# Layer 1 of a two-layer encoder: query rows in natural order, the dilation-16 weights transposed by VectorE in 32x32 blocks, V loaded by class, a new rank table

## The chip, the cores and the metric

The kernel runs on one core of a Trainium2 chip. The metric is device time in microseconds (us) of one launch; the reshaping of inputs and outputs by the host isn't in it. The engines have short names: PE is TensorE's matmul, PEld its weight load, DVE VectorE, ACT ScalarE, POOL GpSimd, SP the queue that issues most DMA transfers. SBUF is the working memory of 128 partitions, PSUM the memory that matmuls write, in banks of 512 float32 a partition.

## What is computed

A sequence of 512 tokens of width 1024, float32, goes through two layers. Each layer adds a normed token mixer and a normed SwiGLU to `x`. Layer 0 mixes by neighbourhood attention on an 8 x 64 grid; layer 1, which the change edits, by dilated attention:

```python
DIL_GROUPS = ((128, 1), (512, 4), (2048, 16))        # window, dilation; 16 heads of 64
for g, (window, dil) in enumerate(DIL_GROUPS):
    radius = window // (2 * dil)                       # 64 in each group
    # queries and keys of one residue mod dil form a sub-sequence of length s // dil
    o, lse = banded_attention(q * HEAD_DIM ** -0.5, k, v, radius, slopes * dil)
alpha = softmax(stack(lses), axis=0)                   # merge the three groups by their denominators
o = einsum('gbsh,gbshd->bshd', alpha, stack(outs))
return o @ w_o
```

With 512 tokens, dilation 4 has four classes (residues) of 128 tokens, and dilation 16 has sixteen of 32 tokens. A dilation-16 class lies within one dilation-4 class. Scores outside the window or of another class get -1e30 and so weight 0.

## The kernel before

**Products.** Every large product is a Winograd scheme with seven products in place of eight (class `Seven`, line 527 on). An operand is split into a high and a low fp32r part (`split`, lines 484 and 485: ACT copies, DVE subtracts), and three matmuls (`mm3`, lines 499 to 501) make one. A unit of layer 1 (`qk_unit`, line 799) makes the queries and keys of one pair of heads `j` (8 pairs) in one group `g` (0, 1, 2 for dilations 1, 4, 16): 24 units. Its weights `r_d` are loaded by the SP queue, their sums are formed by POOL (lines 567 to 573), and its results leave PSUM through `sink` (line 809): step 0 is the first half of the queries (ACT line 812, DVE line 813), step 1 and 2 are the keys (lines 818, 820, 823), step 3 the second half of the queries (ACT line 825). `pieces` says where each part goes: a list of pairs of a destination and a view of the source.

**Row order.** In group 0 the queries are stored in four blocks of 128 tokens, rolled by 64 tokens, and in each block by residue: 32 rows of residue 0 mod 4, 32 of residue 1, and so on (`q4`, line 1324). Hence the source is read with a stride of four, in three pieces per half. In groups 1 and 2 queries and keys are stored by residue mod 4 and in a class by position (`by_token`, line 1310). The rows of attention output and of the final result have the order of group 0, and the host undoes it.

**Attention of layer 1.** For a pair `j` the scores come in chunks. `scores_a` serves dilation 1, `scores_b` (line 1408) both dilated groups: for each class `c` one 128x128 product for dilation 4 and one for dilation 16, side by side. `softmax_pair` adds the bias (custom DVE operation, line 1381) and takes the exponential (ACT, line 1382). The row statistics of the two halves lie in different row orders, so `send` and `swapped` (lines 1340 to 1355) pass them through a small DRAM tile `sw`: one transfer there, four back. `weights` makes the merge factors (lines 1364 to 1372). `weighed` (line 1464) scales the weights by them (ACT, line 1469), transposes eight 128x128 blocks per head and half on PE (line 1479, against `ident`) into two PSUM banks, and copies one bank to SBUF by ACT, one by DVE (line 1480). `values` (line 1482) multiplies V: line 1488 for dilation 1, line 1494 for the dilated groups, which add to the same PSUM bank `o`, 64 partitions per head. `keep` splits and stores the result (lines 1169 to 1172). V itself is made before, stored to DRAM as `vd` and loaded by quarters of four heads (`v_load`, line 1453, transfer in line 1457). After the last pair the output product `yo` follows, and `load_block` (line 1565) loads the residual rows in the order of group 0.

**Order of the work.** The program is written unit after unit (`run`, `between`, `done`): chunks of scores and of `weighed` and `values` of earlier pairs are put between the products of the current unit. The order on each engine isn't the written one. `Order.pin` (line 370) plans it: it schedules the instructions by rank with a table of costs, forward and backward, twenty times, takes the ranks of turn `FIRST`, and then changes ranks by `TABLE`. An entry `(what, engine, lo, hi, turn, by)` names instructions by planned start time or by index, and shifts their ranks. The resulting order is pinned for every engine and for all of the program, so one table ranks layer 0, both feed-forward parts and layer 1. Engines and DMA queues work strictly in this order.

## Time and profile before

| | |
|---|---|
| runs | 1437.45, 1436.01, 1437.60 us; median 1437.45 |
| profiled execution, own time | 1437.08 us |
| its span, first to last instruction | 1435.3 us |
| PE, DVE, ACT, POOL busy | 1393.2, 1190.4, 913.8, 532.0 us |
| TensorE clock granted, mean | 0.994 |
| layer 1's units and attention | about 700 to 1045 us of the span |

Busy is the time in which an engine worked on at least one instruction. A matmul's duration in a group of instructions includes its passage through the array, during which the next ones run; what a run of them costs is read from the distance of their starts or from the chain. The chain that ended last is followed back from the last instruction, at each step to what released it.

### The profile page before, as it was taken

What the parts mean: (1) busy time and instruction counts of PE and PEld (TensorE: products, weight loads), DVE (VectorE), ACT (ScalarE), POOL (GpSimd) and SP (SyncE); (2) the same over time, 40 slices, a digit from 0 to 9 for tenths busy, and PEclk for the clock granted to TensorE, in tenths of its full rate; (3) what the DMA queues carried; (4) which work ended last, traced back from release to release, by engine and by line L of the source; (5) the groups of instructions that cost most, each with busy time, mean ns of one, the idle gap of its engine ahead of it and who ended that gap; (6) DMA issues with size and microseconds to landing.
All of it is one profiled execution on the core that took longest, in us unless ns stands there. A gap on an engine that the chain in (4) does not pass through costs nothing.

```text
span 1435.3 us, 27816 instructions
## 1 busy us (share of the span) xinstructions
PE 1393.2 (97%) x10714; PEld 1301.9 (91%) x10714; DVE 1190.4 (83%) x1891; ACT 913.8 (64%) x1853; POOL 532.0 (37%) x394
## 2 busy tenths in 40 slices
PE   8999999999999999999999999999999999999997
PEld 7989978999999888999999999989988999999886
DVE  7789968899998888998688777777759888898986
ACT  6489965555555667745567787788775645455664
POOL 3745526454330001676453334343216443440001
PEclk9999999999999999999999999999999999999999
DMA  7257588778324674455333353433766897845662
GB/s 248 95 200 185 175 294 224 233 227 219 118 91 141 211 234 169 157 170 187 120 103 91 112 171 97 142 96 91 251 200 240 243 250 221 247 127 169 198 213 96
DMA packets 86646, 253.21 MB, mean 176 GB/s; under 512 B 19313, under 2 KB 31601, under 8 KB 84465
## 3 DMA queue, kind: packets, MB, share of 16 engines
q1 hardware_dynamic: 77696, 197.69, 41.5%
q0 software_dynamic: 8672, 53.48, 14.8%
q8 instruction: 84, 1.38, 0.4%
q14 instruction: 50, 0.40, 0.1%
q10 hardware_dynamic: 144, 0.26, 0.0%
HBM read 229.24 MB, written 68.29 MB: 207 GB/s over the span
## 4 chain that ended last, share of the span: by engine, by line
PE 77%; DVE 12%; ACT 4%; issue 3%; DMA 2%; POOL 1%; POOLq 0%; DVEq 0%; SPq 0%; ACTq 0%
PE gu L499 8%; PE gu L501 8%; PE gu L500 8%; PE pp_d L499 5%; DVE wring L485 4%; PE pp_d L501 4%; PE pp_d L500 4%; PE yd_s L499 3%; PE yd_s L500 3%; PE yd_s L501 3%; PE yd_pp L500 2%; PE yd_pp L499 2%; PE yd_pp L501 2%; PE yo L501 2%; PE yo L499 2%
## 5 line engine op out<-in xcount | busy, mean ns | idle before, releaser
L499 PE MATMUL gu<-rxa,wring 128*128 128x256 f32 x704 | 193.6, 281 | 1.5 <-DVE mem L978 1.3
L501 PE MATMUL gu<-rxa,wring 128*128 128x256 f32 x704 | 190.4, 278 | 2.2 <-DVE wring L485 2.2
L500 PE MATMUL gu<-rxa,wring 128*128 128x256 f32 x704 | 192.3, 277 | 0.0
L485 DVE TENSOR_TENSOR wring<-r_d,wring 128x1024 fp32r<-128x1024 f32 x112 | 142.9, 1283 | 39.9 <-ACT wring L484 39.2
L485 DVE TENSOR_TENSOR wring<-raw,wring 128x1024 fp32r<-128x1024 f32 (+1 forms) x120 | 156.0, 1302 | 16.8 <-ACT wring L484 16.2
L484 ACT ACTIVATE wring<-raw 128x1024 fp32r<-128x1024 f32 x120 | 122.4, 1020 | 61.2 <-PE gu L500 31.2
L484 ACT ACTIVATE wring<-r_d 128x1024 fp32r<-128x1024 f32 x112 | 115.8, 1040 | 33.2 <-PE gu L500 9.5
L499 PEld LDWEIGHTS gu<-rxa,wring 128*128 128x128 f32 x704 | 131.3, 188 | 4.5 <-DVE mem L978 2.3
L501 PEld LDWEIGHTS gu<-rxa,wring 128*128 128x128 f32 x704 | 130.3, 188 | 3.3 <-DVE wring L485 3.2
L500 PEld LDWEIGHTS gu<-rxa,wring 128*128 128x128 f32 x704 | 131.9, 188 | 0.2
L499 PE MATMUL pp_d<-rxa,wring 128*128 128x256 f32 x384 | 108.2, 284 | 2.4 <-ACT wring L484 0.9
L500 PE MATMUL pp_d<-rxa,wring 128*128 128x256 f32 x384 | 106.6, 280 | 0.0
L501 PE MATMUL pp_d<-rxa,wring 128*128 128x256 f32 x384 | 105.5, 280 | 0.0
L707 POOL TENSOR_TENSOR rs_yd<-v_yd,consts 128x1 f32<-128x1 f32 x8 | 8.9, 1115 | 259.2 <-DVE v_yd L705 259.2
L499 PE MATMUL gu<-rxc,wring 128*128 128x256 f32 x352 | 98.5, 282 | 5.2 <-ACT wring L484 3.3
L500 PE MATMUL gu<-rxc,wring 128*128 128x256 f32 x352 | 99.0, 282 | 1.4 <-DVE rxc L724 1.4
L501 PE MATMUL gu<-rxc,wring 128*128 128x256 f32 x352 | 98.7, 282 | 0.4 <-DVE wring L485 0.3
L484 ACT ACTIVATE wring<-r_gu 128x1024 fp32r<-128x1024 f32 x60 | 63.5, 1058 | 50.6 <-PE gu L500 23.5
L484 ACT ACTIVATE rxc<-mem 128x512 fp32r<-128x512 f32 (+2 forms) x95 | 60.6, 645 | 52.2 <-PE yd_pp L500 21.1
L485 DVE TENSOR_TENSOR wring<-r_gu,wring 128x1024 fp32r<-128x1024 f32 x60 | 76.9, 1284 | 13.2 <-ACT wring L484 12.9
L567 POOL TENSOR_TENSOR r_d<-r_d 128x512 f32<-128x512 f32 x24 | 34.0, 1415 | 132.2 <-DVE wring L485 97.2
L567 POOL TENSOR_TENSOR r_gu<-r_gu 128x512 f32<-128x512 f32 x20 | 33.8, 1692 | 127.7 <-DVE wring L485 92.8
(477 smaller groups left out, 5240.7 us busy)
## 6 DMA issues: line engine op xcount, KB each, us to landing
wsum<-wd POOLq DMA_DIRECT2D x24, 1408.0 KB, 10.8
r_d<-dil_qk SPq DMA_DIRECT2D x48, 512.0 KB, 4.0
raw<-wg SPq DMA_DIRECT2D x24, 512.0 KB, 6.0
raw<-wu SPq DMA_DIRECT2D x24, 512.0 KB, 8.3
wsum<-wsum POOLq DMA_DIRECT2D x8, 1408.0 KB, 7.9
raw<-wsum SPq DMA_DIRECT2D x22, 512.0 KB, 4.3
r_gu<-wg SPq DMA_DIRECT2D x20, 512.0 KB, 5.9
r_gu<-wu SPq DMA_DIRECT2D x20, 512.0 KB, 8.4
```

Of the source, the lines that this page charges most:

```text
L484: act.activation(h, src, AF.Copy)
L485: dve.tensor_sub(l, src, h.bitcast(F32))
L499: i = pe.matmul(o, s[0], m[0], start=start, stop=False, skip_group_check=True)
L500: pe.matmul(o, s[0], m[1], start=False, stop=False, skip_group_check=True)
L501: pe.matmul(o, s[1], m[0], start=False, stop=stop, skip_group_check=True)
L567: self.added = e[0].tensor_add(q[0], q[0], q[2])
L707: pool.tensor_tensor(r, v, mhalf, op=ALU.pow)
```

## The change

It does six things, all but the last in layer 1.

1. Group 0 stores its queries in natural order: one piece in the first half, two in the second. Groups 1 and 2 store a dilation-4 class of 128 rows as four runs of 32, one for each residue of the position mod 4 (`p r s a`: class, run, place). Their queries' sum in step 0 is made in four DVE instructions in place of one (`pairs`).
2. With that order each dilation-16 class is a run of 32 rows and of 32 columns, so the 128x128 block of weights is zero off its four 32x32 diagonal blocks. Its transpose is the transpose of each 32x32 block in its own place, for which `dve.transpose` is called, SBUF to SBUF: four of them per head in place of four PE transposes, one PSUM bank and one DVE copy. Dilation 4 and dilation 1 stay on PE.
3. The dilated value products write the bank `o` in natural token order: for a class, columns with a stride of 16 in place of runs of 32.
4. `v_load` loads V of the two dilated groups in four transfers of 32 partitions each, one for each run.
5. `swapped` passes the statistics through a tile of 512 rows of four values: one transfer of small pieces and four by run, in the one direction or the other. `load_block` loads two pieces of 64 rows in place of four or eight pieces. The bias arrays have other contents and the same shape; the host's reordering of the output goes.
6. `FIRST` and `TABLE` are replaced whole.

```diff
-FIRST, TABLE = 2, (
-    (0, 5, 957181, 993986, 6, 279), (0, 5, 741028, 748810, 14, 3080), (2, 0, 10189, 10217, 0, -1138),
...
+FIRST, TABLE = 11, (
+    (0, 5, 49788, 92169, 1, -42768), (2, 5, 5932, 6125, 0, -961), (2, 5, 7102, 7152, 0, -1660),
...
+        def pairs(o, v):
+            return [(o, v)] if len(o.shape) < 4 else [(o[:, :, n], v[:, :, n]) for n in range(o.shape[2])]
+
...
-                sums = in_turn([dve.scalar_tensor_tensor(o, view(left), 0.125, o, op0=ALU.mult, op1=ALU.add)
-                                for o, view in qd[0]])
+                sums = in_turn([dve.scalar_tensor_tensor(o, v, 0.125, o, op0=ALU.mult, op1=ALU.add)
+                                for o, view in qd[0] for o, v in pairs(o, view(left))])
...
-        return v.rearrange("p (m r) -> p r m", r=4)
+        return v.rearrange("p (a s r) -> p r s a", s=4, r=4)
...
-            q4 = qs.rearrange("p (b r n) -> p b r n", b=4, r=4)
-            qd = [[(q4[:, 0, :, 16:], places(0, 16)), (q4[:, 1], places(16, 32)), (q4[:, 2, :, :16], places(48, 16))],
-                  [(q4[:, 2, :, 16:], places(0, 16)), (q4[:, 3], places(16, 32)), (q4[:, 0, :, :16], places(48, 16))]]
+            qd = [[(qs[:, 64:320], whole)], [(qs[:, 320:], some(whole, 0, 192)), (qs[:, :64], some(whole, 192, 64))]]
...
-            q3, k3 = (v.rearrange("p (r n) -> p r n", r=4) for v in qk[i])
-            qd = [[(q3[:, :, 16:80], by_token)], [(q3[:, :, 80:], places(0, 48)), (q3[:, :, :16], places(48, 16))]]
-            kd = [[(k3[:, :, 64 * n:64 * n + 64], by_token)] for n in range(2)]
+            q3, k3 = (v.rearrange("p (r s a) -> p r s a", s=4, r=4) for v in qk[i])
+            qd = [[(q3[..., 4:20], by_token)], [(q3[..., 20:], some(by_token, 0, 12)), (q3[..., :4], some(by_token, 12, 4))]]
+            kd = [[(k3[..., 16 * n:16 * n + 16], by_token)] for n in range(2)]
...
+    sw = [dpool.tile([SEQ, 4], F32, name=f"sw{i}") for i in range(4)]
+    def swapped(out_, in_, d, back):
+        rows = d.rearrange("(b p) k -> p b k", b=4)
+        by_class = d.rearrange("(a s r) k -> s a (r k)", s=4, r=4)
+        if not back:
+            nc.sync.dma_start(rows, in_.rearrange("p (b k) -> p b k", b=4))
+        for n in range(4):
+            v = slice(32 * n, 32 * n + 32)
+            nc.sync.dma_start(*((by_class[n], in_[v]) if back else (out_[v], by_class[n])))
+        if back:
+            nc.sync.dma_start(out_.rearrange("p (b k) -> p b k", b=4), rows)
...
-            nc.sync.dma_start(v, src.rearrange("(t p) c -> p t c" if g == 0 else "(p t) c -> p t c", t=NT))
+            if g == 0:
+                nc.sync.dma_start(v, src.rearrange("(t p) c -> p t c", t=NT))
+            else:
+                for n in range(4):
+                    nc.sync.dma_start(v[32 * n:32 * n + 32], src.rearrange("(a s r) c -> s a r c", s=4, r=4)[n])
...
-        for n in range(2):
+        for i in range(4) if a_b else ():
+            dve.transpose(pt[:, 512 + i * P:512 + i * P + P], part(*b8[4 + i]))
+        for n in range(2 - a_b):
             t = bank("t", f"t1_{j}")
...
-                    pe.matmul(o[64 * hd:64 * hd + 64].rearrange("p (b r n) -> p b r n", b=4, r=4)[:, :, c],
+                    pe.matmul(o[64 * hd:64 * hd + 64].rearrange("p (a s r) -> p r s a", s=4, r=4)[:, c],
...
     def load_block(xt, b):
...
+        nc.sync.dma_start(xt[:64], spill[1][(b + 3) % 4, 64:])
+        nc.sync.dma_start(xt[64:], spill[1][b, :64])
```

More of the change, by code (lines that the diff above doesn't have):

```diff
@@ L1310, in by_token, with some @@
     def by_token(v):
-        return v.rearrange("p (m r) -> p r m", r=4)
-    def places(i, n):
-        return lambda v: by_token(v)[:, :, i:i + n]
+        return v.rearrange("p (a s r) -> p r s a", s=4, r=4)
+    def some(view, i, n):
+        return lambda v: view(v)[..., i:i + n]
     xm, qk, us = mixer_operands(rxb), {}, {}
@@ L1330, in unit_of @@
             qk[i] = next(f_), next(f_)
-            q3, k3 = (v.rearrange("p (r n) -> p r n", r=4) for v in qk[i])
-            qd = [[(q3[:, :, 16:80], by_token)], [(q3[:, :, 80:], places(0, 48)), (q3[:, :, :16], places(48, 16))]]
-            kd = [[(k3[:, :, 64 * n:64 * n + 64], by_token)] for n in range(2)]
+            q3, k3 = (v.rearrange("p (r s a) -> p r s a", s=4, r=4) for v in qk[i])
+            qd = [[(q3[..., 4:20], by_token)], [(q3[..., 20:], some(by_token, 0, 12)), (q3[..., :4], some(by_token, 12, 4))]]
+            kd = [[(k3[..., 16 * n:16 * n + 16], by_token)] for n in range(2)]
         us[i] = qk_unit((a["dil_qk"][g, 0, j], a["dil_qk"][g, 1, j]), xm, next(p5_), next(w22_), f"d{i}", (qd, kd))
         return us[i]
-    sw = [dpool.tile([P, 16], F32, name=f"sw{i}") for i in range(4)]
-    def swapped(out_, in_, d, n):
-        nc.sync.dma_start(d[:, :4 * n], in_)
-        for k in range(4):
-            nc.sync.dma_start(out_[32 * k:32 * k + 32].rearrange("p (i s) -> p i s", s=n),
-                              d[:, n * k:n * k + n].rearrange("(i p) s -> p i s", i=4))
+    sw = [dpool.tile([SEQ, 4], F32, name=f"sw{i}") for i in range(4)]
[9 more added lines that the diff above has]
+            nc.sync.dma_start(out_.rearrange("p (b k) -> p b k", b=4), rows)
     def by_kind(v):
@@ L1354, in send @@
         few = stats[j][2]
-        swapped(few[:, 48 - 16 * t:64 - 16 * t], stats[j][t], sw[2 * t + j % 2], 4)
+        swapped(few[:, 48 - 16 * t:64 - 16 * t], stats[j][t], sw[2 * t + j % 2], t)
     def weights(j):
@@ L1565, in load_block @@
     def load_block(xt, b):
-        rows = spill[1].rearrange("t (m r) d -> r (t m) d", r=4)
-        for r in range(4):
-            if b:
-                nc.sync.dma_start(xt[32 * r:32 * r + 32], rows[r, 32 * b - 16:32 * b + 16])
-            else:
-                nc.sync.dma_start(xt[32 * r:32 * r + 16], rows[r, 112:128])
-                nc.sync.dma_start(xt[32 * r + 16:32 * r + 32], rows[r, 0:16])
+        nc.sync.dma_start(xt[:64], spill[1][(b + 3) % 4, 64:])
+        nc.sync.dma_start(xt[64:], spill[1][b, :64])
     then(exp, AF.Exp)
@@ L1617, in _dist @@
 def _dist():
-    r, n = np.divmod(np.arange(P), 32)
-    q = (4 * n + r)[:, None]
     k = np.arange(P)
+    q = k[:, None]
     dp, dn = np.abs(q + 64 - k), np.abs(q - 64 - k)
     prev, next_ = np.where(dp <= 64, -dp, NEG), np.where(dn <= 64, -dn, NEG)
-    d = 4 * np.abs(k[:, None] - (k + 16) % P)
+    n, a = np.divmod(k, 32)
+    m = 4 * a + n
+    d = 4 * np.abs(m[:, None] - (m + 16) % P)
     return np.concatenate([prev, next_, np.where(k < 64, NEG, prev), np.where(k < 64, next_, NEG),
@@ L1668 @@
     y = r.results[0]["out"]
-    return np.ascontiguousarray(y.reshape(4, 4, 32, D).transpose(0, 2, 1, 3).reshape(1, SEQ, D))
+    return np.ascontiguousarray(y.reshape(1, SEQ, D))
```

121 rows, old and new, of the table c are left out of this document.

## The prediction, made before the changed kernel was run

> **What bounds the kernel now.** I read the first part of the profile page first, then busy time by stage, because the change touches only layer 1's mixer and an average over the span says little of it.
>
> ```profile
> PE 1393.2 (97%) x10714; PEld 1301.9 (91%) x10714; DVE 1190.4 (83%) x1891; ACT 913.8 (64%) x1853; POOL 532.0 (37%) x394
> PE 77%; DVE 12%; ACT 4%; issue 3%; DMA 2%; POOL 1%; POOLq 0%; DVEq 0%; SPq 0%; ACTq 0%
> ```
> ```profile
> core 0: us, PE busy (x) PEld busy (x) DVE busy (x) ACT busy (x) POOL busy (x), PEclk, DMA share, GB/s
> 245.00:560.00 315.00, 310.77 (x2266) 292.39 (x2265) 280.73 (x361) 182.44 (x303) 87.20 (x56) 0.99 0.59 185
> 700.00:765.00 65.00, 62.42 (x528) 60.44 (x527) 52.61 (x89) 40.76 (x94) 33.78 (x24) 1.00 0.38 112
> 765.00:1045.00 280.00, 274.11 (x2474) 258.03 (x2474) 214.11 (x510) 222.48 (x586) 101.31 (x75) 1.00 0.43 135
> 1045.00:1075.00 30.00, 30.00 (x180) 24.32 (x179) 14.13 (x22) 19.99 (x38) 3.06 (x3) 1.00 0.64 186
> ```
>
> The first line of the page is busy time by engine, the second the chain that ended last by engine. TensorE (PE) is busy 97% of the span and carries 77% of the chain. In the stages that the change touches, 700 to 1075 us, it is busy 62.42 + 274.11 + 30.00 = 366.5 of 375 us: 8.5 us idle. VectorE (DVE) is busy 214 of 280 us in the main stage, so 66 us are open there; ScalarE has 57. The row 245 to 560 shows a stage in which DVE is busy 280.73 of 315 us (89%) and PE still 98.7%. So in this kernel a microsecond taken from PE inside 765 to 1045 comes off the end, and work given to DVE is paid only where it delays PE.
>
> **The transposes that leave TensorE.** Per head and weight half the kernel transposes eight 128x128 blocks on PE and copies two banks out, one by ScalarE (ACT), one by DVE. In the dilated half the second bank (dilation 16) goes to DVE altogether: 16 heads x 4 = 64 transposes leave PE, 16 DVE copies go, 64 DVE transposes come.
>
> ```profile
> L1479 PE MATMUL t<-ident,mem 128*128 128x128 f32 x256 | 38.0, 274 | 1.2 <-ACT mem L1469 1.2
> L1480 DVE COPY mem<-t 128x512 f32<-128x512 f32 x32 | 22.0, 689 | 20.1 <-PE t L1479 19.9
> L1494 PE MATMUL o<-mem 128*64 128x128 f32 x256 | 17.2, 274 | 0.0
> ```
> ```profile
> 823.14 0.87 PE t L1479 x8
> 829.36 1.75 PE o L1494 x32
> 921.95 6.46 DMA r_d<-dil_qk
> 1204.99 9.02 DMA raw<-wg
> ```
> ```profile
> 822.75 0.28 PE L500 MATMUL pp_d<-rxa,wring 128*128 128x256 f32 x1
> 822.87 0.28 PE L501 MATMUL pp_d<-rxa,wring 128*128 128x256 f32 x1
> 822.98 1.04 PE L1479 MATMUL t<-ident,mem 128*128 128x128 f32 x8
> 823.82 0.39 PE L499 MATMUL pp_d<-rxb,rxc 128*128 128x256 f32 x1
> 824.05 0.28 PE L500 MATMUL pp_d<-rxb,rxc 128*128 128x256 f32 x1
> ```
>
> The group's mean of 274 ns is a latency; matmuls are pipelined. What a transpose costs PE is read from the chain (second fence): eight take 0.87 us, 109 ns each. Hence 64 x 0.109 = **-7.0 us**. The timeline in the third fence gives the change between kinds of matmul: from 822.87 to 824.05 are 1.18 us, which hold two ordinary steps of 0.12 us (822.75 to 822.87 is one) and the eight transposes, so 1.18 - 0.24 - 0.87 = 0.07 us for going in and out. Where the second bank was a visit of its own that goes too: 16 x 0.07 = 1.1 us at most, nothing at least; I take half, **-0.6 us**.
>
> On DVE 16 x 0.689 = 11.0 us leave. No DVE transpose stands in the trace. The nearest rows are operations of 64, 128 and 256 elements a partition:
>
> ```profile
> L813 DVE SCALAR_TENSOR_TENSOR memc<-pp_d,memc x24: 207/214/281, 694.0 to 1019.8; 128x64 f32<-128x64 f32 x16, 128x128 f32<-128x128 f32 x8
> L813 DVE SCALAR_TENSOR_TENSOR mem<-pp_d,mem x16: 407/418/445, 707.9 to 1005.3; 128x256 f32<-128x256 f32 x16
> L820 DVE TENSOR_TENSOR mem<-mem,pp_d x16: 405/418/422, 721.1 to 1013.3; 128x256 f32<-128x256 f32 x16
> L823 DVE TENSOR_TENSOR mem<-memc,pp_d x16: 496/609/702, 725.5 to 1015.5; 128x256 f32<-128x256 f32 x16
> L823 DVE TENSOR_TENSOR memc<-memc,pp_d x8: 406/415/421, 708.9 to 1032.3; 128x256 f32<-128x256 f32 x8
> L818 ACT ACTIVATE mem<-pp_d x16: 364/384/387, 720.2 to 1012.9; 128x256 f32<-128x256 f32 x16
> L818 ACT ACTIVATE memc<-pp_d x8: 366/383/385, 705.0 to 1029.3; 128x256 f32<-128x256 f32 x8
> ```
>
> The slowest of the first row, 281 ns, is its 128-element form. Bounds for a transpose: 214 ns (the 64-element form) and 689 ns (the 512-element copy). I take 281, the row of the same size: 64 x 0.281 = 18.0 us, at the ends 13.7 and 44.1. So DVE gains 7.0 us, at worst 33. The Trainium skill, "VectorE: DVE Perf Modes", section "The three transpose paths", gives 311 ns for a 128x128 bf16 block on VectorE, whose blocks of 32x32 are transposed each in its place; by it DVE would gain 8.9 us in place of 7.0, and no run here shows it. The new DVE transposes wait for ACT's scaling of the weights; behind them on DVE stand the weight splits of L485, which PE's products need. Before, a copy stood there that waited for the same scaling and then for PE (19.9 us in all for both halves), so no wait is added and about half of one goes; its gain on PE is counted at nothing, since the stage's PE has little idle time to give.
>
> **Query sinks.** For dilation 1 three pieces become one in the first half and two in the second: per head pair DVE goes from 214 + 281 + 214 to one operation of 418 ns, -0.29 us; ACT loses three instructions. For the two dilated groups the DVE sum is cut in four because of its four-dimensional pattern: 4 x 214 in place of 418 ns, +0.44 us, 16 times. Together 16 x 0.44 - 8 x 0.29 = +4.7 us of DVE. With the transposes that is +11.7 us: 226 of 280 us, still under the 89% of the stage shown above. Strides grow from 4 to 16 elements in the dilated reads. In the rows of L818 and L820 against the contiguous L823 `memc` row, reading PSUM with the stride of 4 costs nothing (384 against 383, 418 against 415 ns); a strided SBUF operand costs (609 against 415), and is strided already. I take 0. The sum is also 0.44 us later for whoever needs the `left` bank: if every one of 16 were exposed, +7.0 us; none, 0.
>
> ```profile
> PEld pp_d L499 <- DVE mem L813: 0.2, 1, 0.2
> POOL r_d L567 <- DMA r_d<-dil_qk: 22.2, 4, 10.5
> ```
>
> In the list of waits PE's weight loads waited once for this line, 0.2 us. Cover is there (scores and values stand between), so I take two exposures: **+0.8 us**.
>
> **The value products** write the same columns to PSUM with a stride of 16 elements in place of runs of 32. No matmul of the trace writes so. L1494 takes 1.75 us per head pair (32 records, two column halves side by side): 16 records in line, 109 ns each for 128 columns, 0.85 ns a column. The bounds are 0 (the same columns through the same array, nothing makes them shorter) and a doubling, 8 x 1.75 = +14.0 us, more than the factor 1.47 that a strided SBUF operand costs DVE. ACT reads strided PSUM without loss at (384 - 226)/192 = 0.82 ns an element (226 is the 64-element row of L812 below), a new line of PSUM each time; that is as fast as these matmuls write. I take 0. The Trainium skill says the contrary, "Advanced Engine Details and Errata", section "PSUM Cachelines": a pattern that isn't contiguous slows matmuls significantly. By it the sum would lose the most of what it gains; it is the first rival below.
>
> **DMA.** Each quarter of V loads two dilated groups in four transfers each in place of one: +24, six of these loads inside 700 to 1075. The swap of statistics keeps five transfers and as many packets (512 of 16 bytes, 128 of 64), only the direction of the small ones differs. The residual rows lose 12.
>
> ```profile
> L1457 SPq DMA_DIRECT2D mem<-vd x9: 337/383/958, 829.6 to 1019.6; - x9
> mem<-spill SPq DMA_DIRECT2D x12, 128.0 KB, 2.9
> mem<-vd SPq DMA_DIRECT2D x9, 512.0 KB, 4.7
> mem<-sw SPq DMA_DIRECT2D x64, 2.0 KB, 3.0
> L812 ACT ACTIVATE memc<-pp_d x24: 201/226/277, 693.0 to 1018.7; 128x64 f32<-128x64 f32 x16, 128x128 f32<-128x128 f32 x8
> ```
>
> An issue costs the SP queue 0.383 us. A quarter's load puts 6 more ahead of whatever follows, 2.3 us; three quarters come in the stage, 6.9 us if PE stood for all. Queued behind are the weight loads `r_d`, and POOL already waited 22.2 us for them; the chain has one such load on it (921.95, 6.46 us, just behind a V load). Transfers of 128 KB on 32 partitions land in 2.9 us (the residual rows), four against one of 4.7 us. I take **+0.5 us**. For the swap I take 0: the trip is about 2.9 + 3.0 us and a unit of products (84 matmuls of 0.12 us) covers 10; a doubled landing would still be hidden in the middle pairs and exposed only for the last, where PE has the output product. The 12 issues saved lie under a PE that is busy 30.00 of 30 us: 0.
>
> **The order.** The new table re-ranks the whole program, layer 0 and both feed-forward parts too. PE idles 1435.3 - 1393.2 = 42 us; a new order can win or lose some of it. I take 0, with 4 us to either side: the loads that stand on the chain cost it 6 to 9 us each, and most of their time PE has other work.
>
> **Sum:** -7.0 - 0.6 + 0.8 + 0.5 = -6.3 us. The profiled execution took 1437.08 us (span 1435.3), 0.4 below the median of 1437.45: **1430.8 us**, or 0.44% less. Its own range: 1424.5 (both banks' switching, -8.1, half of the stage's 8.5 us idle closed) to 1434.5 (half of the late sinks exposed, +2.7, and 1 us more of issues).
>
> **Rivals.**
> 1. *Strided PSUM writes slow the value products; slower.* One mechanism, at L1494: with a factor f on its 14.0 us the total is 1430.8 + 14.0 (f - 1). The gain is gone from f = 1.45; at the doubling, 1444.8. For it: no row shows a strided matmul write, and adding to PSUM reads and writes. Against: the strided reads of L818 above. 15%, of which 4 with an f too small to cost the whole gain.
> 2. *No gain, the stage is held elsewhere.* Weight splits on ACT and DVE and the loads of `r_d` set the pace; the holes in PE grow by what it was given: about 1437, with the order's 4 us from 1435 to 1441. For it: 12% of the chain is DVE. Against: 8.5 us of idle PE in 375. 12%.
> 3. *DVE becomes the bound:* transposes at 689 ns, DVE at 214 + 33 + 5 = 252 of 280 us (90%), like the stage shown at 89% where PE still keeps 98.7%. PE would lose 1 to 2% more of 280 us: 1434 to 1437. 5%.
> 4. *A load comes late in the new order:* the six added issues stand before `r_d`, or the table places a weight load late; one more hole of 6.5 to 9 us as at 921.95 and 1204.99: 1437 to 1440; two of them, 1444 to 1449. 4% each.
>
> Forecast: 60%. About 0.2%, 2.9 us, is what a measurement of this kernel tells from no change. Faster: 57 of the 60, 4 of rival 1, 3 of rival 3: 64%. Within: 3 + 3 of rival 1 + 8 of rival 2 + 2 of 3 + 4 of 4 = 20%. Slower: 8 + 4 + 4 = 16%. The range that leaves 2 in 10 out reaches to 1422 below (the forecast's lower end with an order that wins 2.5) and 1442 above (rival 1 to f = 1.8, rivals 2 and 3 whole, rival 4 with one hole).
>
> **What will show it.** L1479 with 192 records in place of 256; 64 DVE transposes near 281 ns; PE busy some 7 us less over the span and the mixer's stage shorter by that. Wrong if the 32 records of L1494 take clearly more than 1.75 us (rival 1), if PE's idle time between 700 and 1075 grows by 5 us or more (rivals 2 and 3), if a wait of PE for L813 or of POOL and ACT for `r_d` grows by microseconds (late sinks, rival 4), or if a stage that was not edited moves by more than 4 us.

## The result: 1.65% slower

The changed kernel took 1460.95 us (median; 1458.22 to 1464.29), the kernel before 1437.53 us on the same chip: 1.0165 times, 95% interval 1.0141 to 1.0188, 23.4 us more. The forecast was 1430.8 us, its range ended at 1442. The profiled execution has a span of 1459.8 us, against 1435.3.

The first part of the page of the changed kernel, busy time by engine, and its chain:

```profile
PE 1401.4 (96%) x10650; PEld 1304.1 (89%) x10650; DVE 1200.5 (82%) x1971; ACT 911.0 (62%) x1829; POOL 548.9 (38%) x394
PE 17%; DVE 4%; DMA 2%; issue 1%; ACT 1%; POOL 1%; POOLq 0%; DVEq 0%; SPq 0%; ACTq 0%
```

What matters is PE: 64 matmuls fewer than before (10650 against 10714), and 8.2 us *more* busy time (1393.2 before). More work can't be the reason; a slower clock can be a part of it, which the last section takes up. The shares of this page's chain add up to 26%, those of the kernel before to 99%: here the page follows the chain over a part of the span only, so I read it by windows, below.

What was edited behaves as foreseen. The groups of the four edited operations, with count, busy us and mean ns:

```profile
L1490 DVE STREAM_TRANSPOSE mem<-mem 128x128 f32<-128x128 f32 x64 | 15.9, 288 | 2.5 <-ACT mem L1482 2.1
L1494 PE MATMUL t<-ident,mem 128*128 128x128 f32 x192 | 36.2, 283 | 2.1 <-ACT mem L1482 2.0
L1495 DVE COPY mem<-t 128x512 f32<-128x512 f32 x16 | 11.0, 689 | 10.0 <-PE t L1494 10.0
L1509 PE MATMUL o<-mem 128*64 128x128 f32 x256 | 18.5, 275 | 0.0
```

192 transposes are left on PE, DVE has 64 at 288 ns (281 was assumed), 16 copies are gone, and the value products with the strided PSUM write keep their 275 ns. The edited mixer's stage, in the stretches that the prediction used:

```profile
700.00:765.00 65.00, 64.11 (x548) 62.28 (x547) 47.51 (x98) 40.44 (x88) 34.42 (x23) 1.00 0.35 107
765.00:1045.00 280.00, 270.99 (x2378) 253.52 (x2377) 223.66 (x561) 215.94 (x550) 111.58 (x78) 0.99 0.47 129
1045.00:1075.00 30.00, 30.00 (x184) 24.81 (x183) 17.77 (x44) 22.40 (x50) 0.66 (x2) 1.00 0.74 210
```

PE idles 9.9 us of these 375, after 8.5 before. The stretches are fixed in time and the changed kernel reaches its work later, so they show how busy the stage is and not how long it takes. Nothing here is 23 us. So I looked where each stage begins and ends, by the first and last matmul of its PSUM tile. Here the gate and up products `gu` of both layers, before and after: shortest, median and longest in ns, then the start of the first and of the last. Layer 0's first is in the row of `rxc`, layer 1's last in the row of `rxa,wring`.

```profile
L501 PE MATMUL gu<-rxa,wring x704: 276/276/388, 257.6 to 1327.1; 128*128 128x256 f32 x176
L499 PE MATMUL gu<-rxc,wring x352: 276/276/420, 240.7 to 1299.4; 128*128 128x256 f32 x176
```
```profile
L504 PE MATMUL gu<-rxa,wring x704: 276/276/417, 265.2 to 1351.9; 128*128 128x256 f32 x176
L502 PE MATMUL gu<-rxc,wring x352: 276/276/581, 249.0 to 1322.3; 128*128 128x256 f32 x176
```

Layer 0's mixer, of which no line was edited, hands over at 249.0 in place of 240.7. The same reading of the other tiles gives the lengths of the stages:

| stage, us | before | after | difference |
|---|---|---|---|
| start to first `gu` (layer 0's mixer, not edited) | 240.7 | 249.0 | +8.3 |
| to the first product of the dilated V, `vp_d` (layer 0's feed-forward part, not edited) | 333.1 | 329.5 | -3.6 |
| to the last transpose `t` (layer 1's mixer, edited) | 492.6 | 498.9 | +6.3 |
| to the last `gu` (second gate and up, not edited) | 260.7 | 274.5 | +13.8 |
| to the last product `yd_s` of the second down stage (not edited) | 99.6 | 99.6 | 0 |

18.5 of 24.8 us arose where only the rank table acts. Two places make most of them. By windows (columns: PE, PEld, DVE, ACT and POOL busy, then PE's granted clock, the transfer engines' share, GB/s), before and then after:

```profile
130.00:160.00 30.00, 29.76 (x249) 27.58 (x250) 27.32 (x75) 28.06 (x74) 13.93 (x18) 1.00 0.66 180
1110.00:1150.00 40.00, 39.90 (x343) 39.25 (x342) 36.07 (x50) 24.01 (x42) 19.60 (x13) 1.00 0.78 226
1150.00:1200.00 50.00, 49.69 (x432) 49.31 (x431) 44.61 (x55) 24.55 (x43) 21.89 (x17) 1.00 0.79 222
```
```profile
130.00:160.00 30.00, 26.50 (x197) 23.72 (x195) 23.04 (x67) 20.55 (x57) 13.51 (x14) 0.94 0.58 158
1110.00:1150.00 40.00, 36.73 (x311) 35.71 (x309) 33.15 (x46) 22.69 (x40) 25.51 (x17) 1.00 0.69 202
1150.00:1200.00 50.00, 42.44 (x347) 41.58 (x348) 33.87 (x43) 23.07 (x40) 14.95 (x12) 0.93 0.80 216
```

In 1150 to 1200 the changed kernel issued 347 matmuls where the one before issued 432, and the clock was 0.93. In the first place 249 - 197 = 52 matmuls are missing, in the second (both rows) 775 - 658 = 117. At 0.12 us each, the usual distance of two, that is an estimated 6 and 14 us. The chain of waits of the changed kernel through that place, and PE's timeline across the hole (start, duration, engine, line, operation, and in brackets what it waited for):

```profile
1138.20 15.62 DMA r_gu<-wg
1153.91 1.06 ACT wring L487
...
1156.03 0.21 PE gu L502
...
1158.29 0.12 PE gu L503
...
1173.63 9.30 DMA raw<-wg
```
```profile
1148.33 0.28 PE L503 MATMUL gu<-rxa,wring 128*128 128x256 f32 x1
1155.02 0.58 PE L502 MATMUL gu<-rxc,wring 128*128 128x256 f32 x1 [6.40 <-ACT wring L487]
```

A weight load of 512 KB took 15.62 us to land; PE stood still for 6.4 us; and when it resumed, a matmul came every 0.21 us in place of 0.12 until 1158. The loss is the hole and then the slow restart.

Around both places POOL issues transfers that were not described so far. The down stage needs sums of its weight quarters, and the transfers form them themselves: 32 of them, of 1.4 MB each (16 per layer, `wsum`, in `wd_sums`, line 1010 of the kernel before), half of which add to what is in memory. They run long ahead of the down stage, next to the weight loads of everything else. The transfers issued at 129 to 143 us, before and after (KB each, median us to landing):

```profile
wsum<-wd POOLq DMA_DIRECT2D x1, 1408.0 KB, 13.7
r_n<-na_qk SPq DMA_DIRECT2D x2, 512.0 KB, 8.3
```
```profile
wsum<-wd POOLq DMA_DIRECT2D x1, 1408.0 KB, 13.4
r_n<-na_qk SPq DMA_DIRECT2D x2, 512.0 KB, 11.4
```

In the kernel before SP issues one weight load of `r_n` at 129.13, ahead of the sum at 130.19, and one behind it, at 131.18; in the changed order both go out at 130.78, behind the sum of 129.61. The same view of the second place, 1130 to 1156 us, before and after:

```profile
wsum<-wd POOLq DMA_DIRECT2D x3, 1408.0 KB, 11.8
raw<-wg SPq DMA_DIRECT2D x3, 512.0 KB, 8.7
```
```profile
wsum<-wd POOLq DMA_DIRECT2D x4, 1408.0 KB, 13.7
r_gu<-wg SPq DMA_DIRECT2D x1, 512.0 KB, 15.6
```

There the changed order issues four weight loads within 2.2 us (1137.83 to 1140.01), between three sums of 1129.5 to 1133 and a fourth at 1142.26; they land after 11.3 to 20.6 us. The kernel before spreads six loads over 1133.6 to 1155, between sums of 1117 to 1121 and others from 1145 on; they land after 7.2 to 10.4 us in the median of each kind.

### The profile page after: what moved, and what is told of

Read it like the earlier page. It is cut to its first block, busy times and chain, and to the rows that moved or that the text cites. A ratio compares the mean times of both kernels' runs of the same rounds, so it can differ in the third digit from the quotient of the medians.

```text
span 1459.8 us, 27793 instructions
## 1 busy us (share of the span) xinstructions
PE 1401.4 (96%) x10650; PEld 1304.1 (89%) x10650; DVE 1200.5 (82%) x1971; ACT 911.0 (62%) x1829; POOL 548.9 (38%) x394
## 5 line engine op out<-in xcount | busy, mean ns | idle before, releaser
L488 DVE TENSOR_TENSOR wring<-raw,wring 128x1024 fp32r<-128x1024 f32 x120 | 156.3, 1308 | 19.5 <-ACT wring L487 18.3
L502 PEld LDWEIGHTS gu<-rxa,wring 128*128 128x128 f32 x704 | 132.8, 190 | 8.5 <-DVE mem L982 3.5
L504 PEld LDWEIGHTS gu<-rxa,wring 128*128 128x128 f32 x704 | 131.8, 190 | 4.4 <-DVE wring L488 4.4
L503 PEld LDWEIGHTS gu<-rxa,wring 128*128 128x128 f32 x704 | 133.1, 190 | 0.1
L502 PE MATMUL gu<-rxc,wring 128*128 128x256 f32 x352 | 97.8, 280 | 8.9 <-ACT wring L487 8.4
L503 PE MATMUL gu<-rxc,wring 128*128 128x256 f32 x352 | 97.7, 280 | 0.2 <-DVE rxc L727 0.2
L504 PE MATMUL gu<-rxc,wring 128*128 128x256 f32 x352 | 97.7, 279 | 0.0
L570 POOL TENSOR_TENSOR raw<-raw 128x512 f32<-128x512 f32 x24 | 41.2, 1718 | 126.6 <-DVE wring L488 111.9
```

Of the source, the lines that this page charges most:

```text
L488: dve.tensor_sub(l, src, h.bitcast(F32))
L502: i = pe.matmul(o, s[0], m[0], start=start, stop=False, skip_group_check=True)
L503: pe.matmul(o, s[0], m[1], start=False, stop=False, skip_group_check=True)
L504: pe.matmul(o, s[1], m[0], start=False, stop=stop, skip_group_check=True)
L570: self.added = e[0].tensor_add(q[0], q[0], q[2])
```

## Experiments

Theory after this reading, A: the edit is worth about what was forecast, and the new rank table loses 20 us and more, because it issues weight loads where they share the transfer engines with the sums. Rival B: the edited code itself loses time (its strided writes, its extra transfers), and the stages around it only show the consequences. Rival C: the table loses time on the compute engines, and the loads aren't the cause.

To part code from order, every kernel below has the rank of each instruction written into it, so that the order on each engine can be chosen freely:

```diff
-        for _ in range(times):
-            starts, _, end = self.run(rank, False)
...
-        order = self.run(rank, False)[1]
+        rank = given_ranks(len(self.all))
+        order = [sorted((k for k in range(len(self.all)) if self.engine[k] == e), key=lambda k: (rank[k], k))
+                 for e in range(len(ENGINES))]
```

"Old order" means that all instructions which both kernels have stand on each engine in the order of the kernel before, and the new ones where those stood that they replace. All runs, each against the kernel before on the same chip:

| run | code, order | us | ratio to before [95%] |
|---|---|---|---|
| changed kernel | new, new | 1460.95 | 1.0165 [1.0141, 1.0188] |
| e1 | new, old (writes of the swap spread) | 1446.69 | 1.0049 [1.0030, 1.0068] |
| e2 | old, new | 1474.57 | 1.0241 [1.0221, 1.0261] |
| e3 | new, old (writes of the swap together) | 1440.26 | 1.0022 [1.0009, 1.0036] |
| e4 | as e3, V loads, swap and query sums as few as before | 1434.61 | 0.9973 [0.9962, 0.9985] |
| e5 | as e3, all transposes on PE | 1443.44 | 1.0037 [1.0023, 1.0051] |
| e6 | as e3, query sums in one | 1438.48 | 1.0000 [0.9980, 1.0020] |
| e7 | new, new, no sums of down weights | 1438.72 | 0.9991 [0.9977, 1.0005] |
| e8 | new, old, no sums of down weights | 1436.68 | 0.9973 [0.9958, 0.9989] |
| e9 | new; new order in layer 0 only | 1443.88 | 1.0031 [1.0019, 1.0043] |
| e10 | new; new order up to the second gate and up | 1454.34 | 1.0107 [1.0076, 1.0139] |
| e11 | as e3, V in one transfer | 1460.05 | 1.0138 [1.0121, 1.0156] |
| e12 | as e11, swap in one transfer a side | 1455.12 | 1.0110 [1.0091, 1.0129] |
| e13 | new, new, sums with an eighth of the bytes | 1439.75 | 1.0001 [0.9987, 1.0016] |
| e14 | as e3, V in one transfer from plain rows | 1438.20 | 0.9989 [0.9975, 1.0004] |
| e15 | as e3, swap in one transfer a side | 1438.20 | 0.9987 [0.9972, 1.0002] |

### Code or order: e1 and e2

The edit is the ranks alone: the changed code with the old order, and the code before with the new order.

> The changed code, every instruction that it shares with the kernel before put in exactly the order of the kernel before on each of the five queues; the new instructions stand in the places of those that they replace (a DVE transpose where the PE transpose of the same block stood). Theory A (the loss is the new rank table: stages whose code is the same carry 18 of the 24.5 us, and the edit itself still saves PE work): the layer-0 mixer is back at 241 us, the second gate and up stage at 235 us, and the whole lies at 1427 to 1436 us. Theory B (the edit costs, by strided PSUM writes, smaller transfers or later DVE work, and holds the later stages up too): 1450 to 1461 us, with the second gate and up stage still near 249 us.

> The code before, in the order of the changed kernel (163 of 10250 shared PE instructions are displaced, by 28 places at most, where the removed transposes come back). Theory A: slower than the kernel before by 18 to 31 us, 1455 to 1468, with the same holes as the changed kernel in the layer-0 mixer (first gate and up product near 249 us) and in the second gate and up stage (about 249 us). Theory B: 1434 to 1442 us.

Measured: 1446.69 and 1474.57 us (before: 1439.17). The new order costs the old code 35.4 us. With it, layer 0 hands over at 248.8 us and the second gate and up stage ends at 1365.8: the holes belong to the order, not to the edited lines. In the old order the changed code hands over at 240.9, as before. So most of the loss is the table's; B is left with at most 7.5 us. Neither run lies in a range that was expected: e1 is 11 us over A's and under B's, e2 is 7 us over A's. (The expectations count the second gate and up stage from its own first product: by that count it takes 232.7 us before, 247.0 after, 233.3 in e1 and 248.5 in e2.) The 12 us between +35.4 and +23.4 arise in layer 1's mixer: from the first `vp_d` to the last `t` it takes 511.3 us in e2 and 498.9 in the changed kernel, for whose code this order was made. So an edit has no price apart from an order.

In e1 the four class-side writes of a swap back stand on SP's queue where the four small reads of before stood. SP's own waits in the mixer, 700 to 1075 us, have a row for it (us in total, times, longest):

```profile
SPq L1423 <- DMA sw<-mem: 25.3, 9, 4.8
```

SP stands there for the swap's own writes to land (15.6 us in all in the kernel before), and the weight loads stand behind it. e3 takes that up.

### The edit's parts in the old order: e3 to e6

e3 is e1 with the four class-side writes of a swap at the place of the one write of before:

```
SP's queue around one swap, e1:  write, load, write, statistics of the other half, write, write, read, ...
                            e3:  write, write, write, write, load, read, ...
```

> As e1 (changed code, order of the kernel before), but where the swap of statistics has four small writes and one read in place of one write and four reads, the four writes stand together in the place of the one write, so that the queue SP isn't held by the landing of the last. Theory A1 (the 7.5 us by which e1 is slower come from SP: the weight loads behind the swap and behind the V loads are late): 1436 to 1443 us. Theory A2 (they come from DVE, which is given the 64 transposes and 48 more sums, so that the weight splits are late): 1444 to 1448 us, as e1.

Measured: 1440.26 us (before 1438.19), 2.1 more than before. That is 6.4 less than e1 by the medians, 5.4 when each is compared with the kernel before on its own chip, and 3.9 by the ratios. SP's longest waits for these writes, in the same stretch of e3:

```profile
SPq L1421 <- DMA sw<-mem: 15.3, 7, 3.8
```

Where eight times four transfers of 2 KB stand in one queue is worth about 4 to 6 us. This is the right base for what follows: with a decent order the edit costs 2 us, where the forecast had a gain of 6.3.

e5 puts the 64 transposes back on PE:

```diff
-        for i in range(4) if a_b else ():
-            dve.transpose(pt[:, 512 + i * P:512 + i * P + P], part(*b8[4 + i]))
-        for n in range(2 - a_b):
+        for n in range(2):
```

> As e3, with the dilation-16 blocks transposed on PE and copied by DVE as before. If PE bounds the stage, 5 to 9 us slower than e3; if DVE bounds it (theory A2), equal to e3 or faster by up to 5 us.

Measured: 1443.44 us, 3.2 above e3 by medians, 2.2 by the ratios, less than the 5 to 9 expected of a stage that PE bounds. Busy time of the two, e3 and then e5, and e3's stretches of the mixer:

```profile
PE 1391.0 (97%) x10650; PEld 1296.5 (90%) x10650; DVE 1191.6 (83%) x1971; ACT 913.2 (64%) x1829; POOL 533.6 (37%) x394
...
700.00:765.00 65.00, 62.23 (x525) 60.33 (x524) 50.73 (x97) 40.06 (x86) 32.04 (x23) 1.00 0.35 108
765.00:1045.00 280.00, 271.55 (x2429) 253.53 (x2428) 216.87 (x574) 220.51 (x563) 101.48 (x76) 1.00 0.45 133
1045.00:1075.00 30.00, 29.91 (x173) 22.99 (x173) 14.86 (x30) 20.40 (x41) 3.60 (x4) 1.00 0.69 200
```
```profile
PE 1396.9 (97%) x10714; PEld 1303.9 (90%) x10714; DVE 1191.7 (83%) x1923; ACT 914.3 (63%) x1829; POOL 530.0 (37%) x394
```

The transposes do take 5.9 us from PE (1396.9 to 1391.0); by these two runs 2 to 3 us of it come off the end. Their intervals overlap, so this pair alone doesn't tell that from nothing; e4, below, shows a gain of that size. In e3 PE idles 375 - 363.7 = 11.3 us in these stretches, 2.8 more than in the kernel before: with all parts of the edit in, some of what PE was given it spends waiting.

e6 undoes the cut of the query sums in four, e4 also the V transfers and the swap. In both the sums' or the transfers' result lies in other places than the class order wants, so the dilated groups' rows are placed wrongly; the work is the same.

```diff
-            return [(o, v)] if len(o.shape) < 4 else [(o[:, :, n], v[:, :, n]) for n in range(o.shape[2])]
+            return [(o, v)] if len(o.shape) < 4 else [(o.rearrange("p r s a -> p (r s) a"), v)]
```
```diff
-                for n in range(4):
-                    nc.sync.dma_start(v[32 * n:32 * n + 32], src.rearrange("(a s r) c -> s a r c", s=4, r=4)[n])
+            nc.sync.dma_start(v, src.rearrange("(t p) c -> p t c" if g == 0 else "(p t) c -> p t c", t=NT))
```

> As e3, with three parts undone: V in one transfer per dilated group, the swap in its old form, and the sum of the dilated queries in one DVE instruction over a view of the same size (left out: with these the rows of V, the statistics and the dilated queries land in other places, so the attention of layer 1 is another one; the amount of work is the same). What stays is the natural row order, the strided PSUM writes and the transposes on DVE. If the transposes' 7 us of PE are worth what the forecast says, 1429 to 1434 us; if taking them from PE is worth nothing because DVE holds the stage, 1436 to 1442 us.

> As e3, with the dilated queries' sum in one DVE instruction in place of four (left out: the rows of the dilated queries land permuted). Theory A2: 3 to 7 us faster than e3. Theory A1: within 1.5 us of e3.

Measured: e6 1438.48 and e4 1434.61 us. From e3 the one sum gives 1.8 us by medians, 3.2 by the ratios (0.8 was forecast for the cut; the intervals of e3 and e6 overlap, so the size isn't settled), and the fewer transfers 3.9 more by either (0.5 was forecast). What remains in e4, the transposes with everything else at the old cost or, for the queries of dilation 1, a little under it, gains 3.6 us on the kernel before (0.27%, interval 0.15 to 0.38%), just outside the 1429 to 1434 us that were expected if the transposes bring their full 7 us.

The value products of e3, in its chain, against 1.75 us before:

```profile
827.90 0.87 PE t L1563 x8
831.98 1.75 PE o L1578 x32
```

The strided PSUM write costs nothing that shows here. With that and with e3 at +2.1 us, B falls as the explanation of the 23.

### The sums, or the order by itself: e7 and e8

The 32 transfers are left out, and the down stages read the weights unsummed; the four sums of the down weights are missing from the result.

```diff
-            after(nc.gpsimd.dma_start(o[:, c], v[:, c], **more), anchor)
...
-        gu, gub, uab, every = (wsum[layer][i] for i in range(4))
+        gu, gub, uab, every = ga, gb, ua, ub
```

> The changed kernel in its own order, with the 32 transfers that add up the down weights in memory left out (16 per layer, 1.4 MB each); the down stages read the weights unsummed, so this kernel leaves those four sums out. If the holes of the new order come from weight loads that share the transfer engines with these sums (the hole at 142 us, the load of 15.6 us in the second gate/up stage), then the first gate/up matmul is back near 240.7 us, the second gate/up stage near 235 us (248.7 in the changed kernel), and the time falls from 1461 to 1441-1446 us. If the order of the loads and of the compute engines makes the holes by itself, it stays at 1455-1462 us, with the stages as in the changed kernel.

> The control: the changed code in the order of the kernel before, the same 32 transfers left out (so the four sums of the down weights are missing here too). With them this order took 1446.7 us. In both theories the sums were hidden here: 1443-1447 us, first gate/up matmul near 240.7 us, second gate/up stage near 235 us.

Measured: 1438.72 and 1436.68 us (before, with its sums: 1439.59), both under what was expected. Without the sums the new order costs 2.0 us more than the old one (2.6 by the ratios); with them it is 20.7 (1460.95 against e3's 1440.26; the kernel before took 1437.53 and 1438.19 beside them). e8's expectation starts from e1; its true sibling is e3, whose placing of the swap it has, so in the old order the sums cost 5 us by medians and 7 by the ratios (1.0022 and 0.9973), in the new one 24 and 25 (1.0165 and 0.9991). The expectation that they are hidden in the old order didn't hold.

The first gate and up products of e7, and its transfers of 129 to 143 us:

```profile
L573 PE MATMUL gu<-rxc,wring x352: 276/276/386, 243.5 to 1300.6; 128*128 128x256 f32 x176
...
r_n<-na_qk SPq DMA_DIRECT2D x2, 512.0 KB, 4.0
```

The two loads that landed in 11.4 us land in 4.0, and layer 0 hands over at 243.5. A's second half is supported: the order by itself is nearly as good as the old, and only together with the sums does it lose. A's first half isn't: the edit was to be worth about 6 us, and in the old order it costs 2 (e3). C keeps the remaining 2 us (5.4 by the two profiled spans, 1438.0 and 1432.6).

### Bytes or issues: e13

The sums' transfers keep their places in POOL's queue and carry an eighth of their columns; the down stages read the weights unsummed as in e7.

```diff
-            c = slice(h * QF, h * QF + QF)
+            c = slice(h * QF, h * QF + QF // 8)
```

> The changed kernel in its own order, with all 32 issues of the sums of the down weights at their places in GpSimd's queue, but each carrying an eighth of its columns (so an eighth of the bytes); the down stages read the weights unsummed, so the sums are missing from the result. Without the issues the new order took 1438.7 us, with them whole 1461. If it is the bytes that the weight loads share the transfer engines with: 1438-1443 us, first gate/up matmul at 243-245 us. If it is the issues (GpSimd's queue, held up by the waits in front of them): 1452-1461 us, first gate/up matmul at 247-249 us.

Measured: 1439.75 us, ratio 1.0001. Its transfers of 129 to 143 us and its gate and up products:

```profile
r_n<-na_qk SPq DMA_DIRECT2D x2, 512.0 KB, 5.3
wsum<-wd POOLq DMA_DIRECT2D x1, 176.0 KB, 3.9
...
L574 PE MATMUL gu<-rxc,wring x352: 275/277/386, 243.6 to 1304.9; 128*128 128x256 f32 x176
```

All issues and waits of POOL's queue are there, and the loss is gone. It is the bytes: the weight loads share the transfers' path with 45 MB of sums. That the transfer engines are full then is seen at the hole of 1148 us, where their share is 1.03 to 1.07 (rows in the last section); whether they or the memory behind them set the limit isn't parted. That the new order issues some loads too shortly ahead of their use for that company is read from the two places above. Loads and sums both moved there, and the new order with only the sums' issues moved was not run, so which of the two moves does it is open.

### Which stage's order: e9 and e10

Ranks of the new order for the instructions up to the end of layer 0 (e9), or up to the second gate and up stage (e10), and of the old order from there on.

```
e9:   new order: layer 0                      old order: layer 1
e10:  new order: layer 0, layer 1's mixer     old order: layer 1's feed-forward part
```

> The changed code; layer 0 in the new order, layer 1 in the order of the kernel before (with which all of it took 1446.7 us). If the new order's loss is made stage by stage where the stage starts late, this has layer 0's part alone: first gate/up matmul 249 us instead of 240.7, the dilated values' first matmul at 578 us instead of 573.8, and a time 4 to 6 us over 1446.7, 1450-1453. If a late layer 0 is what upsets the second gate/up stage (clock, transfers), that stage is longer than 235 us here too and the time is over 1458.

> The changed code; layer 0 and the edited mixer in the new order, everything from the second gate/up stage on in the order of the kernel before. If the 13.8 us that the second gate/up stage gained are made by that stage's own order, they go: 1445-1449 us, stage near 235 us. If they come from the state in which the mixer hands over (what is in flight, the clock after its holes), they stay: 1457-1462 us, stage 245-250 us.

Measured: 1443.88 and 1454.34 us (before 1439.59). Layer 0's new order makes the first `gu` late (248.2, against 240.2 in e3) and costs the whole program 4.3 - 2.1 = 2.2 us over e3 (1.3 by the ratios, with intervals that overlap). Part of its 8 us is given back at once, in layer 0's feed-forward part: at the first `vp_d` 4.8 us are left. Why, was not tested. The base that I named in the expectation was e1's; with e3's the number expected was 1444 to 1446, just missed. In e10 the second gate and up stage takes 266.9 us, neither the 261 of the old order nor the 274.5 of the new: 7.6 us are that stage's own order, about 6 come over its edge. (Counted as in the expectation it takes 238.6 us, between the two numbers there.) What carries them, the transfers in flight or the place of the sums' first transfers, these runs don't tell apart. The time lies between the two expectations.

### The transfers of V and of the swap: e11, e12, e14, e15

These try to keep the edit and drop the 3.9 us. e11 loads V in one transfer to the same partitions, e12 also makes each swap's class side one transfer, e15 does only the latter, and e14 is e11 with plain rows as the source, which leaves the values in other partitions than their classes.

```diff
 e11, e12: V
-                for n in range(4):
-                    nc.sync.dma_start(v[32 * n:32 * n + 32], src.rearrange("(a s r) c -> s a r c", s=4, r=4)[n])
+                nc.sync.dma_start(v.rearrange("p t c -> p (t c)"), src.rearrange("(a s r) c -> s a (r c)", s=4, r=4))
 e14: V
+            nc.sync.dma_start(v, src.rearrange("(t p) c -> p t c" if g == 0 else "(p t) c -> p t c", t=NT))
 e12, e15: swap
-        for n in range(4):
-            v = slice(32 * n, 32 * n + 32)
-            nc.sync.dma_start(*((by_class[n], in_[v]) if back else (out_[v], by_class[n])))
+        nc.sync.dma_start(*((by_class, in_) if back else (out_, by_class)))
```

> The changed code in the order of the kernel before, each load of the dilated values by one transfer again (the same rows of 4 KB go to the same partitions, in the changed class order) instead of four. Four transfers each: 1440.3 us (ratio 1.0022). Both edits of the transfers together cost 3.9 us by the run that undid them. If the count of V transfers carries it: 1436.5-1438, ratio 0.999-1.000. If the swap carries it: 1440, ratio 1.002.

> As the run before, and the four transfers of each swap's class side as one too: two transfers for each swap where both earlier kernels issue five. The three-fold fewer issues leave SP's queue free: 1434-1437 us, ratio 0.997-0.9995, the only version with all of the edit's work that I expect under the kernel before. If issues of the swap are hidden, it is as the run before.

> As e11 (changed code, order of the kernel before, one transfer for each load of the dilated values), but the source of that transfer is the plain row order of the kernel before and not rows picked in four strides; the values then lie in other partitions than the weights' classes, so this part of the result is left wrong. Same bytes, same rows of 4 KB, same count of transfers as e11. If the pattern of the source is what slowed e11 (137 GB/s at 840 to 844 us where four transfers reach 212): 1436-1439 us. If a single large transfer at that place in the queue is slow as such: 1455-1460, like e11.

> Changed code, order of the kernel before, V by four transfers as in the change, each class side of the swap by one transfer instead of four. All four: 1440.3 us. With V in one, this edit of the swap was worth 4.9 us (1460.05 to 1455.12), in a kernel with holes. If the issues on SP's queue carry part of the 3.9 us: 1437-1439 us, ratio 0.999-1.0005. If they are hidden: 1440, ratio 1.002. Over 1443: the one transfer is slow by its pattern, as V's.

Measured: e11 1460.05 us, 20 us *over* e3, a clear miss; e12 1455.12, neither of its two numbers. e14, with as many transfers of as many bytes as e11, 1438.20; e15 1438.20. The stretch behind a V load in e3, then the same and a later one in e11, then e14:

```profile
840.00:844.00 4.00, 4.00 (x36) 4.00 (x36) 2.41 (x6) 3.99 (x12) 2.04 (x2) 1.00 0.85 212
```
```profile
840.00:844.00 4.00, 4.00 (x37) 4.00 (x36) 1.08 (x5) 1.56 (x7) 1.84 (x2) 1.00 0.40 137
...
848.00:852.00 4.00, 4.00 (x22) 3.55 (x22) 2.03 (x2) 1.10 (x2) 0.00 (x0) 0.58 0.58 190
```
```profile
840.00:844.00 4.00, 4.00 (x36) 4.00 (x35) 2.47 (x5) 3.75 (x12) 1.42 (x3) 1.00 0.96 287
```

The source of e11's transfer has an outermost step count of 4 (the four runs of a class), the one of e14 of 128. With 4 the transfer engines were busy 0.40 and moved 137 GB/s, with 128 0.96 and 287 GB/s. Meanwhile loads waited: behind the V transfer of 838.02, e11 issues the next weight load at 843.91 and e14, behind that of 837.58, at 838.47. In 844 to 848 us e11's PE is then busy for 1.73 of 4 us. That the pattern and not the size made e11 slow is shown by e14; that it runs on four engines is what a rule says. The Trainium skill, "DMA: Bandwidth & Descriptors", section "Why a DMA increments its semaphore by 16 and not by 1", has a transfer use the largest number of engines up to 16 that divides the outermost counts of both sides: 4 here, 16 for e14 and for the four transfers of the change (32 rows each). The trace agrees as far as it goes; it doesn't show single engines.

e14 and e15 each lie 0.33 to 0.35% under e3, and their sum is more than e4's 3.9 us, so how the 3.9 divide isn't settled; e15 has all of the edit's work, and against the kernel before it is 0.9987 [0.9972, 1.0002]: no difference that these runs resolve. None of the runs with all of the work is measurably faster than the kernel before.

## Why the prediction was wrong

**The step that failed** is "The order": "I take 0, with 4 us to either side". With e3 as the base the new table costs 20.7 us. Its reason was that most of the time of a late load "PE has other work". That was read from loads on the old chain, in an order that had been fitted around them. It left out that the table moves weight loads against 32 transfers of 1.4 MB, and that PE comes out of a hole at half its clock. The prediction's last sign, "a stage that was not edited moves by more than 4 us", named the failure: +8.3 and +13.8 us.

**Rival 4** ("the table places a weight load late") had the mechanism, with 8%, for one or two holes of 6.5 to 9 us. What came was a hole of 2.8 us at 142 us and one of 6.4 us at 1148 (the load of 15.62 us), each with a slow restart, and smaller waits around them, such as 1.2 us of idle PE behind the load of 9.30 us. It was sized by one or two holes alone, half of it was placed behind the added issues, and the losses arose in stages that had none.

**The transposes**, -7.0 and -0.6: the unit costs were right (DVE 286 to 294 ns against 281; eight PE transposes still 0.87 us), PE's busy time fell by 5.9, but only some 2 to 4 us came off the end (2.2 to 3.2 by e5 against e3, 3.6 by e4). "A microsecond taken from PE inside 765 to 1045 comes off the end" was too strong, by a factor of about two if these sizes hold; PE's idle time grew by 2.8 us, which is rival 2 in part.

**Query sinks**, +0.8: measured 1.8 to 3.2 (e3 against e6); the direction was right, the size probably too small by a factor of two or more, though the two intervals overlap.

**Transfers**, +0.5 for V and 0 for the swap: measured 3.9 together. A slower swap was to "still be hidden in the middle pairs"; but where its four writes stand in SP's queue was worth about 4 to 6 us (e1 against e3). The step counted issues and landings and not what queues behind a swap that waits for its own writes (25.3 us in e1, 15.3 in e3). Its landing for V was short too: the transfers of 128 KB landed after 4.9 us in e3's 690 to 1060 us, not 2.9.

**Strided PSUM writes**, 0: right; 1.75 us per 32 records as before. The rule that was weighed against it, the Trainium skill, "Advanced Engine Details and Errata", section "PSUM Cachelines", doesn't hold for these float32 matmuls with a step of 16 elements. Rival 1 is refuted.

**DVE as the bound** (rival 3): 223.66 of 280 us, against 226 foreseen, in a stage that isn't where the loss arose. Refuted. The Trainium skill's 311 ns ("VectorE: DVE Perf Modes", section "The three transpose paths", for bf16) compare with 288 measured for float32.

Put together in the old order: forecast -6.3, measured +2.1 by medians, +3.2 [+1.3, +5.2] by the ratio. By the medians that part it: transposes -3.2, sums +1.8, transfers +3.9, which make +2.5.

## What to carry to other kernels

When an edit brings a new order for the whole program, the order can be the larger change: price it first, by listing the loads that move against other large transfers, and test it by running old code in the new order and new code in the old one. A load's margin has to be measured with the traffic it will meet (11.4 us in company, 4.0 alone), not with its landing time on an empty queue. And a hole in a busy TensorE costs more than its length, since the restart is slow.

## What was unexpected in the hardware

**The clock after a hole.** The changed kernel's windows around the hole of 1148 us:

```profile
1144.00:1150.00 6.00, 4.04 (x32) 3.84 (x32) 3.28 (x6) 1.73 (x3) 0.00 (x0) 1.00 1.05 265
1150.00:1152.00 2.00, 0.00 (x0) 0.00 (x0) 0.00 (x0) 0.00 (x0) 0.00 (x0) 0.80 1.06 264
1152.00:1155.00 3.00, 0.00 (x0) 0.00 (x0) 0.00 (x0) 1.09 (x2) 0.00 (x0) 0.50 1.03 253
1155.00:1158.00 3.00, 2.98 (x14) 2.98 (x15) 1.89 (x5) 1.76 (x4) 0.00 (x0) 0.50 1.07 264
1158.00:1162.00 4.00, 4.00 (x36) 4.00 (x36) 3.01 (x4) 1.40 (x3) 0.00 (x0) 0.99 0.49 148
```

PE stopped after 1148.33; the granted clock fell to 0.50 some 3 us later and came back some 3 us after PE had resumed: 14 matmuls in 3 us, then 36 in 4. The Trainium skill, "TensorE: Matmul & The Clock Gate", section "Part 1: The HAM clock gate", gives windows of about 3.4 us for both steps; the trace agrees roughly, with some 3 us for each. At 142 us a shorter hole did it too: PE waited 2.76 us and soon after 0.64 us more, and the clock fell when PE had already resumed, to 0.57 over 144 to 148 us. The 1.2 us of idle PE in 1180 to 1184 left it at 1.00. Over the span the mean granted clock was 0.988, against 0.994 before, so 1459.8 x 0.012 - 1435.3 x 0.006 = 8.9 us more of clock withheld; the part of it that fell on waiting PE cost nothing, so this is a bound from above. It can be a part of why PE was busy 8.2 us longer, but not all: 64 matmuls fewer should have made its busy time some 6 us shorter (5.9 from e5 to e3), so about 14 us want a reason. What makes the rest is open.

**Transfers that look alike.** The eight loads of 512 KB for the dilated values, each picked in four strides in place of plain rows, moved a kernel from 1438.20 to 1460.05 us (e14 and e11) at the same count of bytes and issues. How long these loads themselves took to land the trace of e11 doesn't say, but it has what stood behind them. Waits of SP and POOL for transfers in 700 to 1075 us, e11 and then e14 (us in total, times, longest):

```profile
SPq L552 <- DMA mem<-vd: 11.1, 3, 4.8
POOL r_d L639 <- DMA r_d<-dil_qk: 42.1, 5, 12.8
```
```profile
POOL r_d L639 <- DMA r_d<-dil_qk: 18.1, 3, 12.6
```

SP's queue stood for the loads of V before it issued the next weight loads `r_d`, which it did in e14 without such a wait, and POOL then waited 24 us longer for these weights. It was the loads behind V's that came late.
